# Latent attention scores as three products of rounded parts instead of one full-precision product

## The chip, the cores and the metric

One core of a Trainium2 chip runs the whole program. The metric is the device time of one execution in microseconds (us). TensorE (PE) multiplies, VectorE (DVE), ScalarE (ACT) and GpSimd (POOL) work on tiles of 128 partitions in SBUF, and PE writes its sums to PSUM.

## The reference, cut to what matters

The program is a decoder trunk of two layers on 512 rows of 1024 numbers, six sub-layers in this order: feed-forward, latent attention, feed-forward, feed-forward, dilated attention, feed-forward. The change touches the latent attention alone:

```
def mla(h, w_in, q_norm, w_q_up, kv_norm, w_kv_up, w_o):
    lat = h @ w_in                                     # 384 + 256 + 32 columns
    q = (rmsnorm(lat[..., :384], q_norm) @ w_q_up)     # 16 heads x (64 + 32)
    kv = (rmsnorm(lat[..., 384:640], kv_norm) @ w_kv_up)  # 16 heads x (64 + 64)
    q = concat([q[..., :64], rope(q[..., 64:], pos)])
    k = concat([kv[..., :64], broadcast(rope(lat[..., 640:], pos))])
    v = kv[..., 64:]
    s = einsum('bqhd,bkhd->bhqk', q, k) * 96 ** -0.5   # causal, in blocks of 128 queries
    o = softmax(s) @ v
    return o @ w_o
```

So a score is a product over 96 numbers: 64 that belong to the head, and 32 turned by their position, whose key half is the same for all heads.

## The kernel before, in words

Every dense product of the trunk is made of three matmuls (`mm3`, L143 to L145): both operands are kept as a high part, rounded to the type f32r, and a low part, which is what the rounding left, also f32r. The products are high by high, high by low and low by high; the fourth is left out. A weight tile is split by ScalarE (L128, high part) and VectorE (L130, low part); activations are split in a few places in the same way (L759 and L760, and `put_o`, L694 and L695).

The scores of the latent attention are the exception. There the operands are plain f32 tiles of the pool `s` (44 slots of 128 x 512 f32), and one f32 matmul (L862) makes a score tile of 128 queries by n keys, n = 128 (i + 1) for query block i. Its stationary operand is 96 x 128 of `q`, its moving operand 96 x n of `k`.

The operands are made for two heads at a time (e = 0, 1). `key` (L788) runs a projection into a PSUM bank, whose upper 64 partitions are head 0 and lower 64 head 1, copies them by L792 (ScalarE) and L793 (VectorE) into two tiles, and copies the shared turned rows into partitions 64 to 95 of each by L795 (GpSimd, twice). `rope` (L804) does the turned part of the queries of two pairs: a projection, L808 (VectorE shuffle), L809 (VectorE), L810 (GpSimd), L811 (VectorE), then four copies of 32 rows into the query tiles, two by GpSimd (L817) and two by ScalarE (L819). `query` (L798) projects and copies the 64 rows of each head (L802, ScalarE, twice).

`rest` runs this stage. At its start it makes key (0,0), value (0,0), value (1,0), key (0,1), rope (0), query (0,0), value (2,0), one after the other, and then goes through 8 pairs of heads with 4 query blocks each: 32 steps. Each step calls `attend(c, i)`, and after it what the table `BESIDE` names for the step (a key, a query, a rope or a value of a later pair, or a part of the output projection). `attend` puts three pieces into a pipe with a lag of two: `score(i)` at once, `turn(i)` two steps later, `weigh(i)` in the step after. A score is the matmul, a masked minimum by VectorE (L865), the exponential by ScalarE (L868) with its sum, a reciprocal (L871), and the division of the two heads' tiles by VectorE (L873) and ScalarE (L874). `turn` transposes the tiles on TensorE (L890, one matmul per 128 x 128) and copies them out of PSUM (L892, L894, L895); `weigh` multiplies by the values (L904).

Each engine runs its instructions in the order in which they are written; an operation waits until the operations that it depends on have ended, and all behind it on its engine wait too. Weight loads and their splits (L128, L130) are put between the pieces as they come due.

Of the kernel before, what the change touches and what calls it, by code (L numbers as in the profile page):

```python
# [8 lines left out]
F32R = mybir.dt.float32r  # L9
AF = mybir.ActivationFunctionType  # L10
ALU = mybir.AluOpType
# [3 lines left out]
P = 128  # L15
# [24 lines left out]
def f(ap):  # L40
    return ap.bitcast(F32)
# [479 lines left out]
class Ffn:  # L521
# [91 lines left out]
    def rest(self):  # L613
        t = self.t
        last = len(GROUPS) - 1
        for q, (at, n) in enumerate(GROUPS):
            if q == last - 1:
                t.gates(self)
            for ft in range(max(at, START if t.first is self else HEAD), at + n):
                self.head(ft, 0, SEQ)  # L620
                t.pump(3 if t.first is self else 2)
            for i in range(TT if q < last else 0):
                self.down(q, i)
# [76 lines left out]
class Mla(Mixer):  # L700
# [81 lines left out]
    def weight(self, g, ci):  # L782
# [2 lines left out]
            self.wqk[g, ci] = t.weights(t.a[f"mla_qk{ci}"][g])  # L785
        return self.wqk[g, ci]

    def key(self, g, p):  # L788
        t, nc = self.t, self.t.nc
        b = self.project(self.weight(g, 0), 2 * p, (0, 1))  # L790
        k = self.k[2 * g + p] = [t.s() for _ in range(2)]
        nc.scalar.activation(k[0][0:64], b[0:64], AF.Copy)  # L792
        nc.vector.tensor_copy(k[1][0:64], b[64:128])  # L793
        for y in k:
            nc.gpsimd.tensor_scalar(y[64:96], self.lat[2][64:96], 1.0, 0.0, ALU.mult, ALU.add)  # L795

    def query(self, g, p):
        nc = self.t.nc  # L798
        b = self.project(self.weight(g, 1), 3 * p, (3, 4, 5))
        q = self.q[2 * g + p]  # L800
        for e in range(2):
            nc.scalar.activation(q[e][0:64], b[64 * e : 64 * e + 64], AF.Copy)  # L802

    def rope(self, g):  # L804
        t, nc = self.t, self.t.nc
        b = self.project(self.weight(g, 0), 4, (3, 4, 5))
        t1, t2 = t.s(), t.s()
        nc.vector.stream_shuffle(t2, b, [(c + 16) % 32 for c in range(32)])  # L808
        nc.vector.tensor_tensor(t1, b, self.cos, ALU.mult)  # L809
        nc.gpsimd.tensor_tensor(t2, t2, self.sin, ALU.mult)  # L810
        nc.vector.tensor_tensor(t1, t1, t2, ALU.add)  # L811
        for p in range(2):
            q = self.q[2 * g + p] = [t.s() for _ in range(2)]
            for e in range(2):
                r = t1[64 * p + 32 * e : 64 * p + 32 * e + 32]
                if p:
                    nc.gpsimd.tensor_scalar(q[e][64:96], r, 1.0, 0.0, ALU.mult, ALU.add)  # L817
                else:
                    nc.scalar.activation(q[e][64:96], r, AF.Copy)  # L819


    BESIDE = {
# [26 lines left out]
    def attend(self, c, i, pipe):  # L849
        t, nc = self.t, self.t.nc  # L850
# [4 lines left out]
        q, k = self.q[c], self.k[c]  # L855

        def score(i):
            n = (i + 1) * P
            box[i] = []
            for e in range(2):  # L860
                s = t.bank()[:, :n]
                nc.tensor.matmul(s, q[e][0:96, i * P : n], k[e][0:96, :n], start=True, stop=True)  # L862
                p = (t.t("u", UB) if i % 2 else t.t("sq", SB))[:, :n]
                nm, z = st[:, i, e : e + 1], st[:, i, 2 + e : 3 + e]
                nc.vector.tensor_tensor_reduce(  # L865
                    p, s, self.mask[:, SEQ - n :], -sc, 3e38, ALU.add, ALU.min, accum_out=nm
                )
                nc.scalar.activation(p, p, AF.Exp, bias=nm, scale=-1.0, accum_out=z)  # L868
                box[i].append(p)
            r = st[:, i, 4:6]  # L870
            nc.vector.reciprocal(r, st[:, i, 2:4])  # L871
            p = box[i]
            nc.vector.tensor_scalar(p[0], p[0], r[:, 0:1], None, ALU.mult)  # L873
            nc.scalar.activation(p[1], p[1], AF.Copy, scale=r[:, 1:2])  # L874
# [23 lines left out]
        def weigh(i):  # L898
# [13 lines left out]
            if i == 3:  # L912
                self.put_o(box["o"])

        pipe.push(i, score, turn, weigh)

    def rest(self):
        self.t.gates(self)
        self.wv, self.wqk, self.v, self.q, self.k = [], {}, {}, {}, {}
        pipe = Pipe(2)  # L920
        self.key(0, 0)
        self.value(0, 0)
        self.value(1, 0)
        self.key(0, 1)
        self.t.count(99)
        self.rope(0)
        self.query(0, 0)
        self.value(2, 0)
        for c in range(8):
            for i in range(4):  # L930
                if (c, i) == (7, 0):
                    self.t.new_y()
                self.attend(c, i, pipe)
                for name, *args in self.BESIDE.get(4 * c + i, ()):
                    getattr(self, name)(*args)
        for ns in ((3, 4, 5), (6, 7)):
            pipe.step()
            for n in ns:
                self.part(n)
        pipe.flush()  # L940
# [475 lines left out]
```

## Time and profile before

| | us |
|---|---|
| median of 3 runs | 2272.66 |
| lowest and highest | 2272.47, 2272.93 |
| the profiled execution | 2273.08 |
| its span | 2271.3 |
| stage of the latent scores, in the span | 447 to 566 |

The profiled execution is 0.42 us above the median and 1.8 us above its own span. In the rows below, times of a row are its start, counted from the start of the span, and its length; a group such as "x6" is of consecutive instructions of one line, and its length runs from the first start to the last end. Matmuls overlap, so the price of one in a stream is the distance between starts, not its own length. An f32 matmul of L862 leaves two records, so that "x4" of L862 are two matmuls.

### The profile page before, as it was taken

The page shows a single profiled execution, that of the slowest core. Times are in us where ns is not written, and L with a number is a line of the kernel's source. Part 1 is how long each engine was busy: PE and PEld are TensorE (multiplying, and loading weights), DVE is VectorE, ACT ScalarE, POOL GpSimd, SP SyncE. Part 2 cuts the span into 40 slices and gives each one's busy share as a digit, 9 for nine tenths or more (in the row PEclk, how much of TensorE's full clock was granted, in tenths as well). Part 3 has the DMA queues.
Part 4 walks back from the last instruction along what each step waited for, and adds up shares of the span by engine and source line. Part 5 has one row for each costly group of instructions (what it writes and reads, how often), then busy time and mean ns, then how long its engine had stood idle before and what let it go on. Part 6 is the DMA issues. An engine that isn't in the chain of part 4 may idle for free. (4 is left out here: it accounts for less than half of the span.)

```text
span 2271.3 us, 30190 instructions
## 1 busy us (share of the span) xinstructions
PE 2240.5 (99%) x11422; PEld 1851.4 (82%) x11422; DVE 1203.6 (53%) x2712; ACT 861.3 (38%) x1752; POOL 105.2 (5%) x143
## 2 busy tenths in 40 slices
PE   7999999999999999999999999999999999999998
PEld 5888888877898888898888888778878878888887
DVE  7666566677655366474554473334434367243344
ACT  4422135577633132353222352444344346332232
POOL 0000001210110000020000010000000002000000
PEclk9999999999999999999999999999999999999999
DMA  8575662311255365344653523333333332243231
GB/s 307 163 249 180 187 232 68 100 48 57 76 171 180 93 213 173 106 140 127 191 174 114 156 93 105 80 96 87 81 93 87 89 79 80 75 130 100 76 111 38
DMA packets 121224, 284.04 MB, mean 125 GB/s; under 512 B 44130, under 2 KB 48501, under 8 KB 121078
## 3 DMA queue, kind: packets, MB, share of 16 engines
q1 hardware_dynamic: 121078, 282.11, 40.8%
q8 instruction: 89, 1.46, 0.3%
q14 instruction: 57, 0.47, 0.1%
HBM read 279.67 MB, written 2.39 MB: 124 GB/s over the span
## 5 line engine op out<-in xcount | busy, mean ns | idle before, releaser
L143 PE MATMUL mm<-s,whi 128*128 128x512 f32 (+1 forms) x2116 | 796.9, 377 | 3.5 <-ACT whi L128 2.4
L144 PE MATMUL mm<-s,whi 128*128 128x512 f32 (+1 forms) x2116 | 790.9, 374 | 0.0
L145 PE MATMUL mm<-s,wlo 128*128 128x512 f32 (+1 forms) x2116 | 790.5, 374 | 0.0
L128 ACT ACTIVATE whi<-raw 128x1024 fp32r<-128x1024 f32 (+1 forms) x356 | 369.7, 1053 | 962.2 <-PE mm L144 446.6
L130 DVE TENSOR_TENSOR wlo<-raw,whi 128x512 fp32r<-128x512 f32 (+1 forms) x712 | 465.6, 693 | 397.8 <-ACT whi L128 393.8
L143 PEld LDWEIGHTS mm<-s,whi 128*128 128x128 f32 x2116 | 398.7, 188 | 83.4 <-issue 7.0
L145 PEld LDWEIGHTS mm<-s,wlo 128*128 128x128 f32 x2116 | 398.7, 188 | 70.9
L144 PEld LDWEIGHTS mm<-s,whi 128*128 128x128 f32 x2116 | 398.9, 188 | 68.1
L143 PE MATMUL mm<-whi,s 128*128 128x512 f32 x848 | 332.4, 392 | 1.8 <-ACT s L694 1.1
L144 PE MATMUL mm<-wlo,s 128*128 128x512 f32 x848 | 330.4, 390 | 0.0
L145 PE MATMUL mm<-whi,s 128*128 128x512 f32 x848 | 330.1, 390 | 0.0
L165 DVE CUSTOM_DVE_ANT_0 raw<-raw,cs 128x1024 f32<-128x1024 f32 x130 | 159.9, 1234 | 117.7 <-DMA raw<-w_mod 117.2
L143 PEld LDWEIGHTS mm<-whi,s 128*128 128x128 f32 x848 | 159.2, 188 | 36.3 <-issue 2.5
L145 PEld LDWEIGHTS mm<-whi,s 128*128 128x128 f32 x848 | 159.2, 188 | 33.4 <-issue 0.3
L144 PEld LDWEIGHTS mm<-wlo,s 128*128 128x128 f32 x848 | 159.3, 188 | 32.6 <-issue 0.3
L569 DVE TENSOR_TENSOR gg<-silu,mm 128x512 f32<-128x512 f32 (+1 forms) x95 | 60.3, 635 | 171.5 <-PE mm L145 168.3
L459 DVE TENSOR_TENSOR s<-mm,s 128x512 f32<-128x512 f32 x112 | 76.5, 689 | 125.8 <-PE mm L145 125.6
L318 POOL TENSOR_TENSOR mv<-mv,mhalf 128x1 f32<-128x1 f32 x48 | 36.0, 752 | 1498.0 <-DVE mv L317 1495.5
L570 ACT ACTIVATE s<-gg 128x512 fp32r<-128x512 f32 (+1 forms) x97 | 57.4, 591 | 62.0 <-DVE gg L569 62.0
L567 ACT ACTIVATE silu<-mm 128x512 f32<-128x512 f32 (+1 forms) x95 | 51.5, 543 | 31.9 <-PE mm L145 31.9
L1055 ACT ACTIVATE s<-mm 128x512 f32<-128x512 f32 (+3 forms) x156 | 46.2, 373 | 34.8 <-PE mm L145 34.8
L463 ACT ACTIVATE s<-mm 128x512 f32<-128x512 f32 x40 | 23.8, 595 | 85.8 <-PE mm L145 85.5
(168 smaller groups left out, 1737.3 us busy)
## 6 DMA issues: line engine op xcount, KB each, us to landing
raw<-w_gu SPq DMA_DIRECT2D x168, 512.0 KB, 4.3
raw<-w_mod SPq DMA_DIRECT2D x130, 512.0 KB, 4.8
raw<-w_down SPq DMA_DIRECT2D x88, 512.0 KB, 4.3
raw<-dil_in SPq DMA_DIRECT2D x70, 512.0 KB, 3.6
s<-w_mod SPq DMA_DIRECT2D x28, 256.0 KB, 6.3
raw<-w_gu SPq DMA_DIRECT2D x16, 256.0 KB, 3.6
raw<-mla_o SPq DMA_DIRECT2D x8, 512.0 KB, 3.7
raw<-dil_o SPq DMA_DIRECT2D x8, 512.0 KB, 3.6
```

The costliest lines, as they stand in the source:

```text
L128: self.nc.scalar.activation(hi, raw, AF.Copy)
L130: self.nc.vector.tensor_tensor(lo[:, r], raw[:, r], f(hi[:, r]), ALU.subtract)
L143: mm(out, w[0], m[0], start=first, stop=False)
L144: mm(out, w[0], m[1], start=False, stop=False)
L145: mm(out, w[1], m[0], start=False, stop=last)
L165: nc.vector.tensor_tensor_reduce(raw, raw, self.cs, 1.0, 0.0, ALU.mult, ALU.add, accum_out=t[:, 0:1])
L318: nc.gpsimd.tensor_tensor(v[:, 1:2], v[:, 0:1], self.mhalf[:, 0:1], ALU.pow)
L459: nc.vector.tensor_tensor(y, b, y, ALU.add)
L567: nc.scalar.activation(s, banks[0], AF.Silu)
L569: nc.vector.tensor_tensor(v, s, banks[1], ALU.mult)
L570: nc.scalar.activation(ghi, v, AF.Copy)
L1055: nc.scalar.activation(out, src, AF.Copy)
```

## The change

Queries and keys are now kept as high and low parts, and a score is three f32r matmuls into the same bank: high by high, query high by key low, query low by key high (L880 of the changed kernel). The tiles come from the same pool `s`: four for a pair's keys and four for its queries, where there were two and two.

A new function `part_rows` makes the 64 head rows of both heads: three ScalarE copies out of PSUM (two high parts, L793 and L794, and an unrounded copy of head 1, L795) and two VectorE subtractions (L796 reads PSUM and SBUF, L797 two tiles of SBUF). `key` and `query` both call it. The shared turned rows of the keys are split once by `turned_parts` (L821, L822) and copied into each key tile by GpSimd (L805, four a key). `rope` makes one rounded tile of all its rows (L833, ScalarE) and one difference (L834, VectorE) in place of its four copies, and `query` copies 32 rows per head by ScalarE (L813) and by GpSimd (L814).

```
--- before.py
+++ after.py
@@ -785,21 +785,41 @@
             self.wqk[g, ci] = t.weights(t.a[f"mla_qk{ci}"][g])
         return self.wqk[g, ci]
 
+    def part_rows(self, b):
+
+        t, nc = self.t, self.t.nc
+        hi, lo, u = [t.s(F32R), t.s(F32R)], [t.s(F32R), t.s(F32R)], t.s()
+        up, down, r = b[0:64], b[64:128], slice(0, 64)
+        nc.scalar.activation(hi[0][r], up, AF.Copy)
+        nc.scalar.activation(hi[1][r], down, AF.Copy)
+        nc.scalar.activation(u[r], down, AF.Copy)
+        nc.vector.tensor_tensor(lo[0][r], up, f(hi[0][r]), ALU.subtract)
+        nc.vector.tensor_tensor(lo[1][r], u[r], f(hi[1][r]), ALU.subtract)
+        return [hi, lo]
+
     def key(self, g, p):
-        t, nc = self.t, self.t.nc
-        b = self.project(self.weight(g, 0), 2 * p, (0, 1))
-        k = self.k[2 * g + p] = [t.s() for _ in range(2)]
-        nc.scalar.activation(k[0][0:64], b[0:64], AF.Copy)
-        nc.vector.tensor_copy(k[1][0:64], b[64:128])
-        for y in k:
-            nc.gpsimd.tensor_scalar(y[64:96], self.lat[2][64:96], 1.0, 0.0, ALU.mult, ALU.add)
+        nc = self.t.nc
+        k = self.k[2 * g + p] = self.part_rows(self.project(self.weight(g, 0), 2 * p, (0, 1)))
+        for ys, src in zip(k, self.turned):
+            for y in ys:
+                nc.gpsimd.tensor_scalar(y[64:96], f(src[64:96]), 1.0, 0.0, ALU.mult, ALU.add)
 
     def query(self, g, p):
         nc = self.t.nc
-        b = self.project(self.weight(g, 1), 3 * p, (3, 4, 5))
-        q = self.q[2 * g + p]
+        q = self.q[2 * g + p] = self.part_rows(self.project(self.weight(g, 1), 3 * p, (3, 4, 5)))
+        whole, low = self.ropes[g]
         for e in range(2):
-            nc.scalar.activation(q[e][0:64], b[64 * e : 64 * e + 64], AF.Copy)
+            r = slice(64 * p + 32 * e, 64 * p + 32 * e + 32)
+            nc.scalar.activation(q[0][e][64:96], whole[r], AF.Copy)
+            nc.gpsimd.tensor_scalar(q[1][e][64:96], f(low[r]), 1.0, 0.0, ALU.mult, ALU.add)
+
+    def turned_parts(self):
+
+        t, nc = self.t, self.t.nc
+        hi, lo = self.turned = [t.s(F32R), t.s(F32R)]
+        r = slice(64, 96)
+        nc.scalar.activation(hi[r], self.lat[2][r], AF.Copy)
+        nc.vector.tensor_tensor(lo[r], self.lat[2][r], f(hi[r]), ALU.subtract)
 
     def rope(self, g):
         t, nc = self.t, self.t.nc
@@ -809,14 +829,10 @@
         nc.vector.tensor_tensor(t1, b, self.cos, ALU.mult)
         nc.gpsimd.tensor_tensor(t2, t2, self.sin, ALU.mult)
         nc.vector.tensor_tensor(t1, t1, t2, ALU.add)
-        for p in range(2):
-            q = self.q[2 * g + p] = [t.s() for _ in range(2)]
-            for e in range(2):
-                r = t1[64 * p + 32 * e : 64 * p + 32 * e + 32]
-                if p:
-                    nc.gpsimd.tensor_scalar(q[e][64:96], r, 1.0, 0.0, ALU.mult, ALU.add)
-                else:
-                    nc.scalar.activation(q[e][64:96], r, AF.Copy)
+        hi, lo = t.s(F32R), t.s(F32R)
+        nc.scalar.activation(hi, t1, AF.Copy)
+        nc.vector.tensor_tensor(lo, t1, f(hi), ALU.subtract)
+        self.ropes[g] = t1, lo
 
 
     BESIDE = {
@@ -859,7 +875,9 @@
             box[i] = []
             for e in range(2):
                 s = t.bank()[:, :n]
-                nc.tensor.matmul(s, q[e][0:96, i * P : n], k[e][0:96, :n], start=True, stop=True)
+                qs, ks = [x[e][0:96, i * P : n] for x in q], [x[e][0:96, :n] for x in k]
+                for j, (a, b) in enumerate(((0, 0), (0, 1), (1, 0))):
+                    nc.tensor.matmul(s, qs[a], ks[b], start=j == 0, stop=j == 2)
                 p = (t.t("u", UB) if i % 2 else t.t("sq", SB))[:, :n]
                 nm, z = st[:, i, e : e + 1], st[:, i, 2 + e : 3 + e]
                 nc.vector.tensor_tensor_reduce(
@@ -916,8 +934,9 @@
 
     def rest(self):
         self.t.gates(self)
-        self.wv, self.wqk, self.v, self.q, self.k = [], {}, {}, {}, {}
+        self.wv, self.wqk, self.v, self.q, self.k, self.ropes = [], {}, {}, {}, {}, {}
         pipe = Pipe(2)
+        self.turned_parts()
         self.key(0, 0)
         self.value(0, 0)
         self.value(1, 0)
```

On ScalarE the start of the stage stood like this before the change; L780 are the copies of values, L759 the last splits of the normed latents, L128 a weight split, and L868 begins the scores' exponentials.

```order
L780 ACTIVATE s<-mm 128x512
L759 ACTIVATE s<-u 128x256 x2
L792 ACTIVATE s<-mm 64x512
L128 ACTIVATE whi<-raw 128x896
L802 ACTIVATE s<-mm 64x512
L819 ACTIVATE s<-s 32x512 x2
L802 ACTIVATE s<-mm 64x512
L780 ACTIVATE s<-mm 128x512
L868 ACT_TABLE_LOAD
```

The same place on ScalarE after the change, from the value copies to the table load (the first three of L793 to L795 are key (0,1), the second three query (0,0)):

```order
L780 ACTIVATE s<-mm 128x512 x2
L759 ACTIVATE s<-u 128x256 x3
L793 ACTIVATE s<-mm 64x512
L794 ACTIVATE s<-mm 64x512
L795 ACTIVATE s<-mm 64x512
L128 ACTIVATE whi<-raw 128x896
L833 ACTIVATE s<-s 128x512
L793 ACTIVATE s<-mm 64x512
L794 ACTIVATE s<-mm 64x512
L795 ACTIVATE s<-mm 64x512
L813 ACTIVATE s<-s 32x512 x2
L780 ACTIVATE s<-mm 128x512
```

Between the rotated tile of `rope` and the last query copy of pair 0 there stood two L819 and two L802; now there stand L833, L793, L794, L795 and two L813.

On VectorE the same place before, from the last key copy to the rotation of `rope` (0) and the weight split beside it:

```order
L793 COPY s<-mm 64x512
L808 STREAM_SHUFFLE s<-mm 128x512
L809 TENSOR_TENSOR s<-mm,s 128x512
L130 TENSOR_TENSOR wlo<-raw,whi 128x448
L811 TENSOR_TENSOR s<-s 128x512
L130 TENSOR_TENSOR wlo<-raw,whi 128x448
```

And on VectorE after the change, where L796 waits for the third of the three ScalarE copies of its key:

```order
L796 TENSOR_TENSOR s<-mm,s 64x512
L797 TENSOR_TENSOR s<-s 64x512
L828 STREAM_SHUFFLE s<-mm 128x512
L829 TENSOR_TENSOR s<-mm,s 128x512
L130 TENSOR_TENSOR wlo<-raw,whi 128x448
L831 TENSOR_TENSOR s<-s 128x512
L130 TENSOR_TENSOR wlo<-raw,whi 128x448
```

Two subtractions stand ahead of the shuffle where one copy stood.

## Rows read from the trace of the kernel before

**Rows 1.** Page, part 1: busy us, share of the span, instructions.

```profile
PE 2240.5 (99%) x11422; PEld 1851.4 (82%) x11422; DVE 1203.6 (53%) x2712; ACT 861.3 (38%) x1752; POOL 105.2 (5%) x143
```

**Rows 2.** Windows: length, busy us of each engine (instructions), clock, DMA share.

```profile
460.00:500.00 40.00, 40.00 (x258) 29.80 (x256) 29.01 (x93) 28.70 (x72) 5.09 (x7) 1.00 0.23 67
500.00:540.00 40.00, 40.00 (x256) 28.98 (x254) 31.87 (x95) 32.46 (x75) 8.83 (x12) 1.00 0.17 53
```

**Rows 3.** Waits of TensorE, 447 to 566 us: total us, times, longest.

```profile
PE mm L862 <- ACT s L802: 0.8, 1, 0.8
PE mm L862 <- ACT s L819: 0.6, 1, 0.6
```

**Rows 4.** TensorE timeline, 452 to 464 us: start, length, instruction, idle before.

```profile
452.18 1.45 PE L862 MATMUL mm<-s 96*128 96x384 f32 x4
453.47 0.38 PE L890 MATMUL aux<-ident,sq 128*128 128x128 f32 x2
...
455.08 1.88 PE L862 MATMUL mm<-s 96*128 96x512 f32 x4
456.79 0.60 PE L890 MATMUL aux<-ident,u 128*128 128x128 f32 x4
...
458.03 0.39 PE L144 MATMUL mm<-s,whi 128*128 128x512 f32 x1
...
458.96 0.40 PE L145 MATMUL mm<-s,wlo 128*128 128x512 f32 x1
459.19 0.61 PE L862 MATMUL mm<-s 96*128 96x128 f32 x4
459.63 0.82 PE L890 MATMUL aux<-ident,sq 128*128 128x128 f32 x6
...
463.16 1.03 PE L862 MATMUL mm<-s 96*128 96x256 f32 x4
464.03 1.04 PE L890 MATMUL aux<-ident,u 128*128 128x128 f32 x8
```

**Rows 5.** Timeline of TensorE, 408 to 413 us: a stream of 256-wide f32r products.

```profile
408.05 0.28 PE L144 MATMUL mm<-s,whi 128*128 128x256 f32 x1
...
412.13 0.28 PE L145 MATMUL mm<-s,wlo 128*128 128x256 f32 x1
```

**Rows 6.** Timeline of TensorE, where the first scores start.

```profile
446.62 0.39 PE L145 MATMUL mm<-whi,s 128*128 128x512 f32 x1
447.65 0.49 PE L862 MATMUL mm<-s 96*128 96x128 f32 x2 [0.64 <-ACT s L819]
448.92 1.35 PE L862 MATMUL mm<-s 96*128 96x128 f32 x6 [0.78 <-ACT s L802]
```

**Rows 7.** Timeline of ScalarE, key (0,1) to the last query copy of pair 0.

```profile
441.60 0.59 ACT L792 ACTIVATE s<-mm 64x512 f32<-64x512 f32 x1
...
446.97 1.28 ACT L819 ACTIVATE s<-s 32x512 f32<-32x512 f32 x2 [0.69 <-DVE s L811]
448.27 0.59 ACT L802 ACTIVATE s<-mm 64x512 f32<-64x512 f32 x1
```

**Rows 8.** Timeline of VectorE, the rotation of rope (0).

```profile
443.68 0.75 DVE L808 STREAM_SHUFFLE s<-mm 128x512 f32<-128x512 f32 x1
...
444.91 1.42 DVE L130 TENSOR_TENSOR wlo<-raw,whi 128x448 fp32r<-128x448 f32 x1
446.26 0.68 DVE L811 TENSOR_TENSOR s<-s 128x512 f32<-128x512 f32 x1
446.86 0.61 DVE L130 TENSOR_TENSOR wlo<-raw,whi 128x448 fp32r<-128x448 f32 x1
```

**Rows 9.** Timeline of GpSimd, the product of rope (0).

```profile
444.57 1.29 POOL L810 TENSOR_TENSOR s<-s 128x512 f32<-128x512 f32 x1 [4.99 <-issue]
```

**Rows 10.** Instructions of one line: duration in ns, least, median, most.

```profile
L802 ACT ACTIVATE s<-mm x16: 573/594/597, 445.7 to 544.4; 64x512 f32<-64x512 f32 x16
```

**Rows 11.** The same for a copy of turned rows on GpSimd.

```profile
L795 POOL TENSOR_SCALAR s<-s x16: 612/614/748, 427.2 to 532.5; 32x512 f32<-32x512 f32 x16
```

## The prediction

> **What bounds the kernel now.** I read the page's first part first: TensorE is busy 99% of the span, VectorE about half, ScalarE less, GpSimd 5% [rows 1]. The change sits in one stage, so next I cut that stage into windows. From 460 to 540 us TensorE is busy all of both windows of 40 us, at full granted clock; ScalarE is busy 28.70 + 32.46 = 61.2 of 80 us, VectorE 29.01 + 31.87 = 60.9, GpSimd 13.9 [rows 2]. The third view, TensorE's waits from 447 to 566 us, has two lines, 0.6 and 0.8 us, both of the first score matmuls for a query copy of ScalarE [rows 3]; after them it waits for nothing. So three things can change the time: TensorE's own work in the scores, the start of the stage, and ScalarE or VectorE becoming so full that TensorE begins to wait.
>
> **A. The score matmuls.** An f32 matmul leaves two records, so a group "x4" is two of them, and the distance to the next group's start is their price [rows 4]. With 128 keys: 459.63 − 459.19 = 0.44, half is 0.22. With 256: 464.03 − 463.16 = 0.87, 0.435. With 384: 1.29, 0.645. With 512: 1.71, 0.855. A head has one of each, 2.155 us, and 16 heads have 34.5 us.
> An f32r product 512 wide costs (458.96 − 458.03) / 4 = 0.2325 [rows 4], one 256 wide (412.13 − 408.05) / 34 = 0.12 [rows 5]. I put 384 between them at 0.174. No row shows one 128 wide. Bounds: the line through 256 and 512 gives 0.12 − 0.0565 = 0.064 below, and the f32 price of the same width, 0.22, above. I take 0.12, the price of the next width, because the nearest row of 128-wide work with one record each is the transposes, eight in 1.04 us, at most 0.13 each [rows 4].
> Three products of each width are 3 × (0.12 + 0.12 + 0.174 + 0.2325) = 1.94 a head, 31.0 for 16: **−3.5 us**. With 0.064 it is 28.3, −6.2; with 0.22 it is 35.8, +1.3.
> Three matmuls cost less than one here, but only in wide tiles; at 128 keys three of 0.12 lose to 0.22.
> The Trainium skill speaks against the low bound ("TensorE: Matmul & The Clock Gate", LDWEIGHTS (loading the stationary operand)): loading takes about P / 1.2 ns, 107 ns for 128 columns. By it a stream that changes its stationary operand each time can't run below 0.107 us a product, and the term would be about −4.1; no run here shows it for this width, and the transposes agree with it.
>
> **B. The start of the stage.** Before, the last TensorE work ahead of the scores starts at 446.62 and would be over at about 446.85 by the 0.23 of its kind. The first score starts at 447.65, is over at 447.87, and the second head starts at 448.92 [rows 6]: 0.80 + 1.05 = 1.85 us lost. The lost time is the chain key (0,1), rope (0), query (0,0) on ScalarE, VectorE and GpSimd.
> Now that chain with the new instructions, by their order. Key (0,1)'s ScalarE copies began at 441.60 [rows 7]; three of 0.594 [rows 10] end at 443.4, and I allow 0.25 for handing over. L796 waits for the third; L796 and L797 at 0.6 each put the shuffle at 444.85, against 443.68 [rows 8]: 1.17 us late. The rest of the rotation keeps its shape, 3.26 us from the shuffle to the end of the sum (446.26 + 0.68 − 443.68), with the GpSimd product of 1.29 in it [rows 8, 9]: 448.1. On ScalarE L833, priced as a copy of 512 columns at 0.6, ends at 448.7, L793 to L795 at 450.5, the two L813 at 451.1 and 451.7 (0.64 each, as L819 has 1.28 for two [rows 7]). First score 451.1, second head 451.7: 4.25 us lost ahead of the first, and 0.25 between, since three products of 0.12 fill 0.36 of the 0.6. 4.5 − 1.85 is **+2.6 us**. VectorE's low parts go beside this; the third product, which needs the low query, is the one that can come later still. Bounds: +1.4 if the two subtractions ahead of the shuffle delay it by nothing, +4.0 if TensorE waits for both subtractions of the query as well (0.68 each).
> The load of the exponential's table stands behind these copies and moves with them by about three us. The first transposes stood at 453.47 [rows 4] and are themselves asked for 2.6 later. I take nothing for it; it is within the bounds of C.
>
> **C. The stage at pace.** ScalarE loses 8 L792, 16 L802 at 0.594 [rows 10] and 8 L819 at 0.64, 19.4 us, and gains 16 × 3 part copies at 0.594, 16 L813 at 0.64, 4 L833 and L821, 28.5 + 10.2 + 3.0 = 41.7: +22 us. VectorE loses 8 copies and gains 37 subtractions: 29 × 0.68, the length of a 128 x 512 sum [rows 8], +20 us. GpSimd goes from 24 copies (16 L795, 8 L817) to 48: 24 × 0.614 [rows 11], +14.7 us.
> From 460 to 540 there are five queries, five keys and three ropes, by the starts of their lines in the trace. On ScalarE a query gains one part copy and two L813, 1.87; a key two copies, 1.19; a rope loses two copies of 0.64 and gains one of 0.6, −0.68. 5 × 1.87 + 5 × 1.19 − 3 × 0.68 = +13.3: 61.2 + 13.3 = 74.5 of 80 us, 93%. VectorE likewise: 5 × 1.36 + 5 × 0.68 + 3 × 0.68 = +12.2, 73.1 of 80, 91%.
> What covers these instructions is TensorE's own pace. A score is not wanted as weights until the second step after it, and a step is 3 to 4 us (scores start at 452.18, 455.08, 459.19 and 463.16 [rows 4]) with projections in it. What queues behind a late part copy on ScalarE are the exponentials and divisions of the next step, and TensorE's transposes wait for these. I followed the order of ScalarE through these steps with the durations above: it comes out 0 to 3 us ahead of each transposition. So most is hidden; for the places with nothing ahead I take **+2.0 us**. Bounds: 0; and if no idle of ScalarE can be used up, 74.5 + 18.8 = 93.3 against TensorE's 80 − 2.4 = 77.6 (two thirds of A's gain fall in these 80 us), +15.7.
>
> **Sum.** 2273.08 − 3.5 + 2.6 + 2.0 = 2274.2 for an execution like the profiled one, which is 0.42 above the median of the runs; so about **2273.8** for a median.
>
> **The rivals.**
> *ScalarE becomes the bound from 460 to 540 us, slower.* For it: 93% busy, and the idle of before is not free time but waits, for TensorE and VectorE, that come with each step; VectorE at 91% makes these longer, and it is slowed by GpSimd: 1.42 beside L810 against 0.61 [rows 8, 9]. It decides from the point where ScalarE's idle can't fall below 77.6 − 74.5 = 3.1 us. If half of the 18.8 stays, 74.5 + 9.4 = 83.9 against 77.6, 6.3 us of waits in place of 2.0: **2278.1**; with all, 2287.5. Against it: the lag of two steps, and that these waits end when TensorE delivers, which it would do earlier.
> The Trainium skill ("SBUF — State Buffer", Who interferes with whom) states that VectorE and GpSimd share a port pair as an exclusive lock for a whole instruction, the loser blocking fully, among others where VectorE reads two SBUF tiles. The trace agrees in the split of 1.42 us. By it each of the 24 added GpSimd copies could cost VectorE its 0.614, up to 14.7 us, which is weight for this rival and no term of the sum.
> *A 128-wide f32r product costs as much as an f32 one.* The f32 matmul at 128 keys was two records in 0.22; if f32r has no gain at this width, 16 × 3 × 0.10 = 4.8 us on top: **2278.6**. For it: no row shows the width. Against: the transposes at 0.13 [rows 4].
> *Everything is cheap.* The product at 0.064, the start at +1.4, no waits: −6.2 + 1.4 = −4.8, **2267.9**.
>
> **How the numbers follow.** The forecast has 0.50, ScalarE as the bound 0.22, the dear 128-wide product 0.18, all cheap 0.10. 0.2% of 2272.66, about what a measurement of this kernel can tell from no change, is 4.5 us: no change lies from 2268.1 to 2277.2. Faster: half of the cheap case and a little of the forecast's lower side, 0.07. Slower: 0.17 of the ScalarE case, 0.12 of the dear product, 0.06 of the forecast's upper side, 0.35. The same: 0.58. The range leaves out the far half of the cheap case and the upper end of the ScalarE case (up to 2287.5): 2268.5 to 2284. The forecast's own range is 2270 to 2277.
>
> **What would show it.** In the changed profile: L880 in triples at 0.36, 0.36, 0.52 and 0.70 us per head and score; a 128-wide triple at 0.66 is the dear product, at 0.2 the cheap case. The first L880 near 451.1, released by L813 on ScalarE; if its releaser is VectorE or GpSimd, step B named the wrong engine. TensorE's waits from 450 to 566 us with ScalarE or VectorE as releaser and about 2 us in sum; over 6 us is the first rival. ScalarE near 74 of 80 us from 460 to 540; VectorE near 73, more if subtractions stretch beside GpSimd's copies. The forecast is wrong if a wait stands in a stage that it names nowhere: in the output projection after 540 us, where nothing is added but late, or in tiles of the pool not yet free.

## The result: slower by 0.25%

| | before | changed |
|---|---|---|
| median, us (9 runs each) | 2274.84 | 2279.61 |
| lowest and highest | 2272.47, 2276.15 | 2278.90, 2281.21 |
| profiled execution, its span | 2273.08, 2271.3 | 2278.90, 2277.1 |

The ratio is 1.0025, with a 95% interval from 1.0016 to 1.0033. The medians differ by 4.8 us. The forecast was 2273.8, no change, with a range up to 2284: the measured time lies in the range, but above the forecast's own 2270 to 2277, and the difference is just above the 4.5 us that were to count as no change, with an interval (3.6 to 7.5 us) that reaches to both sides of that. The rival in which ScalarE becomes the bound was priced at 2278.1 and lies nearer.

The page of the changed kernel, part 1, beside [rows 1]: TensorE has 1.4 us more, ScalarE 18.9, VectorE 16.7, GpSimd 19.6.

```profile
PE 2241.9 (98%) x11486; PEld 1861.9 (82%) x11486; DVE 1220.3 (54%) x2741; ACT 880.2 (39%) x1789; POOL 124.8 (5%) x167
```

The windows of the start and of the pace, with the columns of [rows 2]. In the first the granted clock is 0.74 of full. From 460 to 540 us ScalarE is busy 72.7 of 80 us and VectorE 70.0; TensorE, which had no gap in [rows 2], is idle 0.8 us.

```profile
447.00:460.00 13.00, 9.22 (x39) 7.98 (x38) 8.00 (x24) 10.98 (x23) 5.21 (x8) 0.74 0.13 42
460.00:500.00 40.00, 39.95 (x285) 32.63 (x285) 34.95 (x107) 37.12 (x91) 10.11 (x13) 1.00 0.18 55
500.00:540.00 40.00, 39.29 (x279) 31.71 (x275) 35.08 (x95) 35.57 (x81) 13.54 (x17) 1.00 0.18 52
```

TensorE's waits, as in [rows 3]. One stands ahead of the first score, and two (1.7 us) later, where the kernel before had none; the releasers are ScalarE and VectorE.

```profile
PE mm L880 <- ACT s L813: 3.8, 1, 3.8
PE aux L922 <- ACT gg L912: 1.1, 1, 1.1
PE aux L922 <- DVE gg L910: 0.6, 1, 0.6
```

TensorE's timeline answers [rows 4] and [rows 6]. The last product starts at 446.87; the first score starts at 451.04, where it was 447.65.

```profile
446.87 0.39 PE L145 MATMUL mm<-whi,s 128*128 128x512 f32 x1
451.04 3.01 PE L880 MATMUL mm<-s 96*128 96x128 f32 x12 [3.78 <-ACT s L813]
453.85 0.63 PE L143 MATMUL mm<-s,whi 128*128 128x512 f32 x1
454.27 0.63 PE L144 MATMUL mm<-s,whi 128*128 128x512 f32 x1
...
457.00 1.22 PE L880 MATMUL mm<-s 96*128 96x384 f32 x6
458.06 0.38 PE L908 MATMUL aux<-ident,sq 128*128 128x128 f32 x2
...
459.65 1.56 PE L880 MATMUL mm<-s 96*128 96x512 f32 x6
461.05 0.60 PE L908 MATMUL aux<-ident,u 128*128 128x128 f32 x4
...
463.45 0.78 PE L880 MATMUL mm<-s 96*128 96x128 f32 x6
464.07 0.84 PE L908 MATMUL aux<-ident,sq 128*128 128x128 f32 x6
...
467.60 0.88 PE L880 MATMUL mm<-s 96*128 96x256 f32 x6
468.32 1.04 PE L908 MATMUL aux<-ident,u 128*128 128x128 f32 x8
```

Read first the spacing of L143 and L144 behind the scores: 454.27 − 453.85 = 0.42 us, where it is 0.2325 in [rows 4]. That is the lower of TensorE's two clock levels, 1.2 in place of 2.4 GHz; the granted clock is low from 449.4 to 456.2 us. Then the prices at full clock, six products to a group: 0.62 / 6 = 0.103 for 128 keys, 0.72 / 6 = 0.12 for 256, 1.06 / 6 = 0.177 for 384, 1.40 / 6 = 0.233 for 512. A head costs 3 × 0.633 = 1.90 us, 16 heads 30.4, against 34.5: −4.1.

ScalarE at the start, beside [rows 7], and VectorE, beside [rows 8]:

```profile
442.70 0.58 ACT L795 ACTIVATE s<-mm 64x512 f32<-64x512 f32 x1
...
448.00 0.63 ACT L833 ACTIVATE s<-s 128x512 fp32r<-128x512 f32 x1 [3.39 <-DVE s L831]
...
449.75 0.58 ACT L795 ACTIVATE s<-mm 64x512 f32<-64x512 f32 x1
450.36 1.28 ACT L813 ACTIVATE s<-s 32x512 fp32r<-32x512 f32 x2
```

```profile
444.54 0.73 DVE L828 STREAM_SHUFFLE s<-mm 128x512 f32<-128x512 f32 x1
...
445.75 1.61 DVE L130 TENSOR_TENSOR wlo<-raw,whi 128x448 fp32r<-128x448 f32 x1
447.29 0.67 DVE L831 TENSOR_TENSOR s<-s 128x512 f32<-128x512 f32 x1
...
450.98 1.09 DVE L797 TENSOR_TENSOR s<-s 64x512 fp32r<-64x512 f32 x1
```

The third part copy of key (0,1) ends at 443.28, the shuffle starts at 444.54 (forecast 444.85), L833 at 448.00, and the two L813 end at 451.64. That is the chain that the prediction worked out, with a first score at 451.1; it came at 451.04. VectorE's last line there, L797, took 1.09 us beside GpSimd's copies.

Since times of whole executions move by 2 to 3 us for reasons that lie outside this stage (last section), I compare kernels by a stretch inside one trace: from the start of the last product ahead of the first score to the start of the last group of weighted values (L904 or L922 with 16 matmuls). It is 580.92 − 446.62 = 134.30 us before, and 585.21 − 446.87 = 138.34 changed: **+4.04**. By the 512-wide score of pair 0 the changed kernel is 4.32 us late (12.78 against 8.46 from the start of the stretch); from there to the end both take the same, 125.6 and 125.8 us, although the score products alone are 3.9 us shorter in that part. So about 3.6 us were lost there, of which 1.7 are the two waits above; the rest is matmuls that start later than at their price without showing an idle, since their records overlap. The sum is +4.5 at the start (4.32, and the 0.2 that pair 0's first scores saved; 3.94 − 1.85 = 2.1 of it is idle, the other 2.4 the lower clock), −4.1 for the products, +3.6 after it.

### The profile page after: what moved, and what is told of

Same layout as the page of the kernel before. It is cut to its first block, busy times and chain, and to the rows that moved or that the text cites. A ratio compares the mean times of both kernels' runs of the same rounds, so it can differ in the third digit from the quotient of the medians.

```text
span 2277.1 us, 30406 instructions
## 1 busy us (share of the span) xinstructions
PE 2241.9 (98%) x11486; PEld 1861.9 (82%) x11486; DVE 1220.3 (54%) x2741; ACT 880.2 (39%) x1789; POOL 124.8 (5%) x167
## 5 line engine op out<-in xcount | busy, mean ns | idle before, releaser
L143 PE MATMUL mm<-s,whi 128*128 128x512 f32 (+1 forms) x2116 | 797.4, 377 | 3.5 <-ACT whi L128 2.3
L144 PE MATMUL mm<-s,whi 128*128 128x512 f32 (+1 forms) x2116 | 792.0, 374 | 0.0
L128 ACT ACTIVATE whi<-raw 128x1024 fp32r<-128x1024 f32 (+1 forms) x356 | 369.7, 1053 | 960.1 <-PE mm L144 438.8
L143 PEld LDWEIGHTS mm<-s,whi 128*128 128x128 f32 x2116 | 399.4, 189 | 84.0 <-issue 7.0
L144 PEld LDWEIGHTS mm<-s,whi 128*128 128x128 f32 x2116 | 399.5, 189 | 68.1 <-DVE s L760 0.7
L143 PE MATMUL mm<-whi,s 128*128 128x512 f32 x848 | 332.3, 392 | 1.6 <-ACT s L694 0.9
L144 PE MATMUL mm<-wlo,s 128*128 128x512 f32 x848 | 330.5, 390 | 0.0
L143 PEld LDWEIGHTS mm<-whi,s 128*128 128x128 f32 x848 | 159.2, 188 | 36.2 <-issue 2.5
L144 PEld LDWEIGHTS mm<-wlo,s 128*128 128x128 f32 x848 | 159.2, 188 | 32.6 <-issue 0.5
```

The source lines that it names most:

```text
L128: self.nc.scalar.activation(hi, raw, AF.Copy)
L143: mm(out, w[0], m[0], start=first, stop=False)
L144: mm(out, w[0], m[1], start=False, stop=False)
```

## The experiments

The table has, from the start of the stretch, the first score, the 512-wide scores of pairs 0, 2 and 4, and the end, in us, and the ratio of the times to before. Each kernel has one trace. The times of `fill` are 3.39 us less than from its last product, the length of the fifteen added ones.

| kernel | first score | pair 0 | pair 2 | pair 4 | end | ratio, interval |
|---|---|---|---|---|---|---|
| before | 1.03 | 8.46 | 40.43 | 72.32 | 134.30 | |
| changed | 4.17 | 12.78 | 43.86 | 74.73 | 138.34 | 1.0025, 1.0016 to 1.0033 |
| fill | 4.15 | 10.96 | 43.71 | 74.58 | 138.22 | 1.0023, 1.0013 to 1.0033 |
| rows_first | 2.44 | 12.28 | 44.26 | 76.39 | 138.56 | 1.0022, 1.0013 to 1.0032 |
| three_alone | 1.03 | 8.17 | 39.13 | 70.01 | 130.22 | 0.9996, 0.9987 to 1.0005 |
| one_product | 4.14 | 11.62 | 42.27 | 71.09 | 132.73 | 1.0007, 0.9998 to 1.0016 |
| no_u | 3.48 | 12.81 | 43.77 | 74.79 | 138.82 | 1.0020, 1.0011 to 1.0029 |
| both | 2.26 | 10.81 | 42.94 | 75.36 | 138.84 | 1.0029, 1.0018 to 1.0041 |
| no_low_rows | 4.18 | 16.65 | 53.10 | 89.49 | 159.01 | one run |
| no_l797 | 3.61 | 12.94 | 43.90 | 74.77 | 137.87 | one run |
| relief | 2.87 | 12.38 | 43.39 | 74.27 | 139.59 | 1.0025, 1.0016 to 1.0034 |
| relief_start | 1.65 | 9.88 | 41.75 | 73.00 | 135.22 | 1.0007, 0.9998 to 1.0016 |
| spread | 4.18 | 13.00 | 44.37 | 77.17 | 140.90 | 1.0032, 1.0021 to 1.0044 |
| spread_all | 2.26 | 10.83 | 42.96 | 77.55 | 139.92 | 1.0032, 1.0020 to 1.0044 |

### Fill: is it the clock?

```
         self.value(2, 0)
+        b = self.t.bank("aux")
+        for k in (0, 1, 0, 1, 0):
+            ls = [x[:, 2 * P : 3 * P] for x in self.latn[k]]
+            self.t.mm3(b, ls, [x[:, :SEQ] for x in self.wv[k]], True, True)
```

> The changed kernel, with fifteen more f32r products of 512 columns on TensorE just ahead of the first score; they repeat a value product into a PSUM bank that nobody reads, so nothing is waited for and nothing is used. Theory of the clock: of the lost time about 2.5 us is TensorE at the lower granted clock after the idle of 3.9 us ahead of the first score. With 15 x 0.23 = 3.45 us of that idle filled, the first score still starts near 451.0, but the clock stays 1.00 from 447 to 460 us, the 384-wide score of pair 0 starts near 454.5 in place of 457.0, and the time falls by 2 to 2.6 us against the changed kernel. Theory of the full ScalarE: its exponentials set the pace of the first steps anyway, so what a full clock gives back returns as waits of TensorE before the first transposes, and the time falls by less than 0.7 us.

TensorE's timeline of this kernel, the same place:

```profile
452.33 2.24 PE L880 MATMUL mm<-s 96*128 96x128 f32 x12 [0.37 <-ACT s L813]
454.41 0.40 PE L143 MATMUL mm<-s,whi 128*128 128x512 f32 x1
...
456.48 1.21 PE L880 MATMUL mm<-s 96*128 96x384 f32 x6
```

The scores and the products behind them run at full clock, 0.23 apart, and the 512-wide score of pair 0 comes 1.8 us sooner. At pair 2 it is 0.15 us sooner, and nothing is left at the end. Between the 512-wide scores of pairs 1 and 2 it was given back, as waits that the changed kernel did not have there (it has none for L780, and one of the two for L910, at 528 us):

```profile
PE aux L922 <- DVE gg L910: 1.2, 2, 0.6
...
PE mm L880 <- ACT s L780: 0.9, 1, 0.9
```

The wait for L780, at 479.43 us, is for a PSUM bank that a value's copy on ScalarE (L780) had not yet emptied, since that copy stood behind the work of the scores. So the lower clock is a loss of TensorE, but not of the kernel: behind the start the other engines were no earlier. The theory of the clock fell: the ratio is 1.0023 for 1.0025, about 0.5 us, where it forecast 2 to 2.6.

### Rows first: a shorter chain at the start

```
-        nc.scalar.activation(hi, t1, AF.Copy)
-        nc.vector.tensor_tensor(lo, t1, f(hi), ALU.subtract)
-        self.ropes[g] = t1, lo
+        self.ropes[g] = t1          # split later, by round_rope(g)
...
         nc.scalar.activation(u[r], down, AF.Copy)
+        if between:                 # query (g, 0): lambda: self.round_rope(g)
+            between()
         nc.vector.tensor_tensor(lo[0][r], up, f(hi[0][r]), ALU.subtract)
```

> The changed kernel, with the order of pair 0 turned: ScalarE copies the part rows of the query (three copies) before it rounds the turned rows of rope, where it sat idle 3.4 us, and VectorE makes the low part of the turned rows before the low parts of the query. Theory of the start (chain and clock): three copies of 0.55 us leave the chain, the first score starts near 449.4 in place of 451.04, the idle ahead of it is about 2.3 us, and the lower clock after it is shorter or gone; the time falls by 1.7 us (clock as before) to 4.2 us (no lower clock). Theory of the full ScalarE: ScalarE has the same instructions to do until the first exponentials, but had 3.4 us idle in front of them; if the pace after that is set by ScalarE and VectorE, TensorE waits later for what it gained here, and the time falls by less than 1 us.

The first score came 1.73 us sooner, as worked out; the low clock stayed as long (6.8 us), and by pair 2 the kernel was 0.4 us behind the changed one. The same answer as that of the fill: the ratio is 1.0022, about 0.7 us less, below the 1.7 to 4.2 of the theory of the start.

### Three alone: the products without the operands

```
-        k = self.k[2 * g + p] = [t.s() for _ in range(2)]
+        k = self.k[2 * g + p] = [t.s(F32R) for _ in range(2)]
...
-                nc.tensor.matmul(s, q[e][0:96, i * P : n], k[e][0:96, :n], start=True, stop=True)
+                for j in range(3):
+                    nc.tensor.matmul(s, q[e][0:96, i * P : n], k[e][0:96, :n], start=j == 0, stop=j == 2)
```

> The kernel before with one thing alone: query and key tiles are of type f32r and a score is three f32r products, all three of the same high parts; no low parts are made, so no instruction of ScalarE, VectorE or GpSimd is added. Term A by the rows of the changed kernel: 3 x (0.103 + 0.12 + 0.177 + 0.233) = 1.90 us a head against 2.155, -4.1 us for 16 heads, and no new waits: the time falls by 3.5 to 4.5 us against the kernel before. Rival, that a shorter score only meets its operands or the exponentials earlier: TensorE waits for ScalarE or VectorE in the stage, and the time falls by less than 2 us.

The stretch fell by 4.08 us: term A is what the rows said, and it is kept when nothing else is added. TensorE's start is as in [rows 6], 0.64 and 0.72 us of waits:

```profile
447.50 0.55 PE L863 MATMUL mm<-s 96*128 96x128 f32 x3 [0.64 <-ACT s L819]
448.77 1.32 PE L863 MATMUL mm<-s 96*128 96x128 f32 x9 [0.72 <-ACT s L802]
...
451.99 1.22 PE L863 MATMUL mm<-s 96*128 96x384 f32 x6
```

The time did not show it (0.9996; a gain of 4.1 us would be 0.9982, outside the interval), so a gain of the stretch is not yet one of the whole kernel: in the profiled execution 1.1 us were given back at 1560 us and 2.2 between 1878 and 1889, where the clock fell, which lies outside the change.

### One product: how far is the floor?

```
-                for j, (a, b) in enumerate(((0, 0), (0, 1), (1, 0))):
-                    nc.tensor.matmul(s, qs[a], ks[b], start=j == 0, stop=j == 2)
+                nc.tensor.matmul(s, qs[0], ks[0], start=True, stop=True)
```

> The changed kernel with the first of the three products alone (high by high); all low parts are still made. TensorE has 20.3 us less to do in the stage (2 x 10.1), the other engines have the same. If ScalarE and VectorE are still covered by TensorE with some room (forecast), the time falls by 15 us or more against the changed kernel. If they are close to setting the pace (rival of the full ScalarE, 72.7 us busy of 80 from 460 to 540), the time falls by 6 to 12 us and TensorE's waits in the stage, for ScalarE and VectorE, grow to 8 us and more.

TensorE had 20.3 us less, and the stretch fell by 5.6. By the ratio the time fell by about 4.1, less than either forecast. The windows show who is full: ScalarE 74.7 of 80 us, VectorE 67.7, while TensorE is idle for 4.9. Behind the first score TensorE's waits are 7.3 us, for ScalarE and VectorE.

```profile
460.00:500.00 40.00, 38.78 (x255) 28.35 (x254) 31.62 (x98) 37.96 (x95) 9.38 (x13) 1.00 0.04 14
500.00:540.00 40.00, 36.30 (x227) 26.95 (x226) 36.06 (x99) 36.77 (x82) 13.99 (x20) 0.91 0.21 67
```

So the other engines hold a floor near 132.7 us, and the changed kernel stands close above it. Up to 3.4 us of this floor are clock: it was granted at the lower level for 3.4 us twice, from 512.4 and from 526.1 us. That other engines come close to setting the pace, as the first rival has it, is shown; which engine it is, is not.

### Without the copy u, and both

```
-        nc.scalar.activation(u[r], down, AF.Copy)
-        nc.vector.tensor_tensor(lo[1][r], u[r], f(hi[1][r]), ALU.subtract)
+        nc.vector.tensor_tensor(lo[1][r], down, f(hi[1][r]), ALU.subtract)
```

> The changed kernel without the unrounded copy of head 1 (L795): VectorE subtracts straight from PSUM for head 1 too. ScalarE has 16 copies of 0.58 us fewer, 9.3 us; VectorE and GpSimd keep their count, and VectorE's L797 has one SBUF operand fewer. The measure is the stretch from the last product ahead of the first score to the start of the last weighted values: 134.3 us before, 138.3 changed, 132.7 with one product. Theory of ScalarE: the waits that came after the start are for things queued on ScalarE (a value's copy that holds a PSUM bank, a copy of transposes, the exponentials); without these copies the waits go, and the stretch falls by 2.5 to 4 us. Theory of VectorE and GpSimd: VectorE is held up by GpSimd's copies and by its own subtractions, and ScalarE only waits for it; the stretch falls by less than 1 us.

> The changed kernel without the unrounded copy of head 1, and with the turned order at the start (part rows of the query before the rounded turned rows). If ScalarE sets the pace, the 1.7 us that the turned order gave at the first score and lost later is kept now, and the low clock after the start is shorter: the stretch from the last product to the last weighted values is 131 to 134 us, below the 134.3 of the kernel before, and the time is level with the kernel before or 1 to 2.5 us below it. If VectorE and GpSimd set it, the stretch stays above 137 us.

ScalarE lost 9.3 us of work and the stretch did not fall (138.82). With the turned order as well, pair 0 came 2.0 us sooner and pair 4 0.6 later (138.84). Neither went as the theory of ScalarE forecast: less work on ScalarE alone gains nothing. VectorE in the second kernel, the window from 500 to 540 us, is busy 37.9 of 40:

```profile
500.00:540.00 40.00, 38.35 (x262) 30.70 (x261) 37.94 (x102) 33.86 (x77) 11.64 (x16) 1.00 0.23 67
```

### GpSimd and VectorE relieved

```
-        nc.vector.tensor_tensor(lo[1][r], u[r], f(hi[1][r]), ALU.subtract)    # no_l797
...
+                    d = 64 if j else 96                                       # no_low_rows
+                    nc.tensor.matmul(s, q[a][e][0:d, i * P : n], k[b][e][0:d, :n], start=j == 0, stop=j == 2)
```

> The changed kernel with GpSimd relieved: the low parts of the 32 turned rows are left out of the second and third product (they run over 64 rows), and GpSimd's 32 copies of them are not made, 20 of its 29.5 us. Theory of VectorE and GpSimd: VectorE's stretched subtractions (1.09 for 0.67) become short, waits go, and the stretch from 138.3 falls by 2 us or more. Theory of ScalarE: it falls by less than 1 us.

> The changed kernel with VectorE relieved: the low part of head 1 is not made (16 subtractions of 0.77 us left out, 12 us), and head 1 uses the low part of head 0 in its place. ScalarE and GpSimd do what they did. Theory of VectorE: the stretch from 138.3 falls by 2 us or more. Theory of ScalarE: by less than 1 us.

The first says nothing on GpSimd: it made TensorE slower by about 20 us, by a price that I had not known (last section). In the second VectorE lost 12 us and the stretch fell by 0.5. So less work on VectorE alone gains little. What GpSimd's copies cost TensorE is left open. What they cost VectorE shows in part in L797, with two operands in SBUF, against L796 with one (columns: busy us, mean ns, then idle before):

```profile
L797 DVE TENSOR_TENSOR s<-s 64x512 fp32r<-64x512 f32 x14 | 10.8, 770 | 0.0
...
L796 DVE TENSOR_TENSOR s<-mm,s 64x512 fp32r<-64x512 f32 x14 | 9.5, 681 | 5.2 <-ACT s L795 5.1
```

The difference, 0.09 us each, is 1.4 us for 16: twelve take 0.67 us and four up to 1.09. It is no bound, since other lines are stretched too; added up over all lines of VectorE, what instructions beside GpSimd took beyond the usual length of their line is an estimated 4.3 us in the stage, where it was 1.2 before. The rule of the Trainium skill that the prediction weighed ("SBUF — State Buffer", Who interferes with whom), a full block for each of the 24 added copies, would be 14.7; the trace shows about 3 more.

### Both relieved, and with the start

> The changed kernel with ScalarE and VectorE relieved at once: no unrounded copy of head 1 (16 ScalarE copies fewer) and no low part of head 1 (16 VectorE subtractions fewer; head 1 uses head 0's). Each alone left the stretch from the last product to the last weighted values within 0.5 us of the changed kernel's 138.3. Theory that the two bound it together, in turn (a score passes VectorE, ScalarE, VectorE and ScalarE before TensorE wants it): the waits after the start go, about 3.4 us, and the stretch is 134.5 to 136. Rival, that something else holds it (a transfer, GpSimd, the PSUM banks): it stays above 137.3.

> The same, with the turned order at the start as well (part rows of the query ahead of the rounded turned rows). If ScalarE and VectorE together were what took back the 1.7 us of that order, it is kept now: the stretch is at least 1.2 us below that of the kernel without the turned order, 132 to 134.5, at or below the 134.3 of the kernel before. Rival: the start is taken back again, and both stand within 0.5 us.

The edits are those of no_u and no_l797 together, and in the second kernel that of rows_first too. The first missed, and lies where its rival put it: 139.59, although pair 4 came 0.5 us sooner than in the changed kernel. It lost in one place. A weight split stands there ahead of a query's copies on ScalarE, which in the changed kernel stands behind them, at 552.75; TensorE waits 1.92 us where that kernel waits 1.12:

```profile
546.31 1.04 ACT L128 ACTIVATE whi<-raw 128x1024 fp32r<-128x1024 f32 x1
550.88 0.43 PE L921 MATMUL aux<-gg,s 128*64 128x128 f32 x2 [1.92 <-ACT gg L911]
```

Then the granted clock was low for 3.4 us from 552.1, which cost an estimated 1.8 us by the prices at full clock; without that the stretch is still 137.8. The second kept what the start gave: 135.22, 3.1 us below the changed kernel and 4.4 below the first, though not in its range of 132 to 134.5, with ScalarE at 34.29 and VectorE at 32.70 of 40 us:

```profile
500.00:540.00 40.00, 39.82 (x274) 32.18 (x273) 32.70 (x93) 34.29 (x79) 12.64 (x17) 1.00 0.17 54
```

Against "both", which differs from it only by the 16 subtractions, it is 3.6 us shorter. The same 16 subtractions gave 0.5 us in no_l797 and −0.8 in the first kernel here. So in these traces VectorE's work costs time once ScalarE has less and the start is early, and not otherwise. That the two bind in turn fits most of these and is not shown; that the place of the weight split is what made the first kernel worse was not tested.

### Spread, and all together

```
-        5: (("query", 1, 0),),
-        6: (("value", 0, 1),),
+        6: (("query", 1, 0),),
+        7: (("value", 0, 1),),
...
-        23: (("key", 3, 1),),
-        24: (("query", 3, 1),),
+        24: (("key", 3, 1),),
+        26: (("query", 3, 1),),
```

> The changed kernel with all its work, and another table of what stands beside each step: each query of a later pair comes one or two steps later, so that no key and query or rope and query of pairs 2 to 7 stand in steps next to each other. If the waits come from what stands together in the queues of ScalarE and VectorE (at 541 to 552 us ScalarE runs through a query and a key without a gap while TensorE waits for a copy behind them), and not from their load over the stage, they shrink, and the stretch falls from 138.3 to 135.5 to 137. If the load over the stage is the cause, it stays above 137.5.

> The changed kernel, the whole computation, with the three edits together: the later queries, no unrounded copy of head 1, the turned order at the start. If load and queue order of ScalarE and VectorE are the cause, the stretch is 132 to 134.5 and the time level with the kernel before. Rival: 137 or more, and the time as that of the changed kernel.

Both came out as the rivals had it: 140.90 and 139.92, 2.6 and 1.6 us more than the changed kernel. A later query is ready only when its pair's first score is asked for: TensorE's waits for L813 are 4.7 us in two places where there was one of 3.8. So a later place of the queries is no cure; an earlier one was not tried. No version was faster than the kernel before by more than the noise.

## Why the prediction was right or wrong

**A, the products: right, better than forecast.** −4.1 against −3.5, because a 128-wide f32r product takes 0.103 us and not the 0.12 of the next width. The rival of the dear 128-wide product (0.22) fell. The Trainium skill's rule ("TensorE: Matmul & The Clock Gate", LDWEIGHTS (loading the stationary operand)), about 0.107 us to load 128 columns, had given −4.1, and the trace is within 4% of it.

**B, the start: the chain right, what follows it missing.** The first score came at 451.04, released by L813 on ScalarE, against 451.1; every link of the chain came within about 0.3 us of its forecast, so this is no luck. TensorE's idle was 3.9 us where 4.5 was forecast, since the stage began 0.25 us later and no gap showed between the two heads. That an idle of 3.9 us is followed by half the clock was put at nothing, without a reason: TensorE's price was 2.4 us, and the term came to +4.5, forecast +2.6, outside its bounds of +1.4 to +4.0. The fill shows that this was not on the path: without it the other engines held the scores back just as far by pair 2.

**C, the stage at pace: mis-sized.** The forecast was 2.0 us of waits, from ScalarE's order followed by hand; 3.6 came. What failed is the sentence that ScalarE comes out 0 to 3 us ahead of each transposition: it followed one engine's queue with the other's answers taken as on time. It held for most of the stage. With the saving of the shorter products added back, the changed kernel is 4.5 us late at the 512-wide score of pair 0 and still 4.6 at the first score of pair 5 (525.50). Then it loses 1.2 us up to 530.82, 0.4 from 541.8 to 546.3, and about 2.0 from 548.8 to 559.9. Each of these places comes behind steps for which the table names nothing (18, 22, and 25 to 27, counted from 0). Such a step takes TensorE 2.4 to 2.5 us (scores start at 519.20 and 521.60, 535.49 and 537.88, 546.27 and 548.77), and not the 3 to 4 that were to cover ScalarE's and VectorE's added work. Behind step 7, the one other such step between the first and the last, 0.1 us is lost here, and in the fill the whole 1.8. They are not the whole of it: rows_first and both lose 1.3 and 1.6 us behind the first score of pair 4 too, where no such step is near. That the short steps are the cause in the changed kernel was not tested by giving them work.

In the first place VectorE is late: it waits 0.77 us for ScalarE's L795, L797 is stretched, and so the copy L910 starts at 527.32, though its transposes were done at 523.7. TensorE wants it:

```profile
524.17 1.02 DVE L797 TENSOR_TENSOR s<-s 64x512 fp32r<-64x512 f32 x1
528.05 0.66 PE L922 MATMUL aux<-gg,s 128*64 128x128 f32 x8 [0.60 <-DVE gg L910]
```

At 549 us, the third place, it is ScalarE. TensorE:

```profile
549.93 0.38 PE L908 MATMUL aux<-ident,sq 128*128 128x128 f32 x2
550.07 0.72 PE L880 MATMUL mm<-s 96*128 96x512 f32 x2
551.91 0.43 PE L922 MATMUL aux<-gg,s 128*64 128x128 f32 x2 [1.12 <-ACT gg L912]
```

and ScalarE there, without a gap:

```profile
548.38 0.59 ACT L794 ACTIVATE s<-mm 64x512 fp32r<-64x512 f32 x1
...
549.49 0.63 ACT L813 ACTIVATE s<-s 32x512 fp32r<-32x512 f32 x1
...
551.05 0.19 ACT L886 ACTIVATION_READ_ACCUMULATOR u<-u,st 128x1 f32 x1
551.26 0.60 ACT L912 ACTIVATE gg<-aux 128x512 f32<-128x512 f32 x1
```

The copy L912 that TensorE wants stands behind a query's three part copies, its L813 and two exponentials, and is 1.12 us late. Before, two copies stood there and no wait. In sum ScalarE's 72.7 of 80 us was forecast at 74.5, VectorE's 70.0 at 73.1: the loads were about right, and what they cost was not.

**The rivals.** "ScalarE becomes the bound" came nearer in time (2278.1) than in mechanism: it priced 6.3 us of waits from 460 to 540 us, where 1.2 came and 2.4 more behind it, and as named, for one engine, it fell, since less work for ScalarE alone gave nothing. "Everything is cheap" fell at the start.

**The whole.** −4.1 + 4.5 + 3.6 = +4.0 in the stage, forecast +1.1: the start was missed by +1.9, the waits by +1.6, the products by −0.6. That the time lies in the range is luck in part, for the range reached that far for the rival in which ScalarE is the bound, and not for the clock or the short steps. The spans differ by 5.8: the rest is 0.25 ahead of the stage and 1.5 behind it, most of it at 1560 and 1906 us, where no instruction was changed, and the experiments show such steps in some executions and not in others. That part is not explained.

## What to carry to other kernels

When TensorE is at 100% and the others look half idle over the whole span, look at the stage: at 76% for ScalarE and VectorE each, in a chain that passes both twice, 19 and 17 us more work on them cost TensorE 8.1 us, against 4.1 that the products saved. Look in it for the steps in which TensorE has little to do, since what it covers elsewhere it may not cover there. Test a suspected bound by taking most of the work from the engine that seems to be it (one product: 20.3 us less for TensorE, 5.6 gained); only then is it known what a saving is worth. A saving at the head of such a stage (1.8 us in the fill) is no gain until it is still there two pairs later.

## What the runs showed of the hardware

Products over 64 rows among those over 96 are dear. In the kernel without the low turned rows, six 512-wide products (96, 64 and 64 rows, twice) took 465.34 − 463.28 = 2.06 us, 0.343 each, where they took 0.233 with 96 rows throughout. By the starts of the single records over the stage, it is not the change of rows alone: the next product starts 0.42 us behind one of 96 rows, 0.34 us from one of 64 rows to another, and 0.32 us from 64 rows to 96. A stream of 64 rows alone was not run.

```profile
463.28 2.13 PE L879 MATMUL mm<-s 96*128 96x512 f32 x6
465.34 0.66 PE L907 MATMUL aux<-ident,u 128*128 128x128 f32 x4
```

An idle of TensorE is followed by a lower clock in some executions and not in others. Near 1900 us, in code that was not changed, before (idle 1.16 and 0.91 us in two windows) the clock stayed at 1.00:

```profile
1895.00:1900.00 5.00, 3.84 (x23) 2.92 (x22) 4.87 (x10) 4.98 (x11) 1.02 (x2) 1.00 0.03 11
1900.00:1906.00 6.00, 5.09 (x39) 4.70 (x38) 5.89 (x12) 5.42 (x14) 2.74 (x3) 1.00 0.50 175
```

and in the changed kernel's execution (idle 1.66 us) it was 0.72 behind it, at the lower level for 3.4 us from 1906.8:

```profile
1900.00:1906.00 6.00, 4.34 (x25) 2.98 (x23) 5.62 (x12) 5.82 (x14) 1.31 (x3) 1.00 0.04 16
1906.00:1912.00 6.00, 6.00 (x38) 6.00 (x39) 5.89 (x11) 5.42 (x13) 3.08 (x3) 0.72 0.64 186
```

Times of the kernel before run from 2272.47 to 2276.15, and this is one place where two traces differ though the code there is the same; how much of that spread comes from it is not shown. That is why an effect of 4 us was read from a stretch of the trace and not from the time alone.
